# Weights in whole blocks, right halves of the last tiles normalised during P4, rotary loads split from their arithmetic

## The chip, the cores and the metric

The kernel runs on one NeuronCore of a Trainium2 chip. The metric is the device time of one execution in microseconds (us). Three timed executions of the kernel before gave 1953.59, 1955.4 and 1960.35 us; the median is 1955.4 us. The engines are named as in the profile: PE (TensorE matmul), PEld (its weight load), DVE (VectorE), ACT (ScalarE), POOL (GpSimd), SP (SyncE, which here issues most DMAs).

## What is computed

One encoder layer on 1024 tokens of width 1024, in float32, with two half-step feed-forward blocks around a mixer that holds two attentions:

```python
h = h + 0.5 * swiglu(rms_norm(h, ffn1_norm), ffn1_w_gate, ffn1_w_up, ffn1_w_down)
u = rms_norm(h, mix_norm)
z = u @ w_in                      # qA|kA|vA|qB|kB|vB|gA|gB, 4352 columns
qb = rope(qb, pos);  kb = rope(kb, pos)
merged = sigmoid(ga) * (ya @ w_branch_a) + sigmoid(gb) * (yb @ w_branch_b)
h = h + merged @ w_out
h = h + 0.5 * swiglu(rms_norm(h, ffn2_norm), ffn2_w_gate, ffn2_w_up, ffn2_w_down)
y = rms_norm(h, final_norm)
```

`ya` is a neighbourhood attention over a 16 x 64 grid and `yb` a windowed attention with a sink; `rope` turns the first five 128-row chunks of the qB and kB columns by tables of cosine and sine. The feed-forward width is 2816.

## The kernel before

**Arithmetic.** Every large product is made in three matmuls of 128x128 by 128x512 (`mm3`, L137): the operands are split into a high and a low part (`split`, L87: an ACT cast makes the high part, a DVE subtraction the low one), and high-high, high-low and low-high are summed in PSUM. The large matrix products are cut by Strassen's scheme into seven products P1 to P7, each of 12 matmuls per 128 rows of output (4 blocks of the contraction times 3).

**Stages.** `hidden` makes gate, up and their product for the first feed-forward block, `Down` its down projection; the same classes serve `w_out` and the second block. Between them a `transition` normalises the eight token tiles and transposes them. The input projection `w_in` runs as `pg`, with five groups of chunks (`groups`, L850); then the two attentions, with gates, branch products and their loads as filler between the units.

**`products` (L253)** walks through a list `seq` of (group, product, m). For product q it first prepares the weights of some products ahead (`prep_until`, L370: three ahead, up to eight later), then issues the 12 matmuls (`multiply`), then takes the result out of PSUM (`leave`, L382, which calls `store_z` for the input projection) and then calls `at_end(len(seq) - 1 - q)`. For `pg` there are 70 products: P1 and P2 of the first three groups (q = 0 to 11), then P5, P6, P3, P7, P4 of group 0 (q = 12 to 21), of group 1 (22 to 31) and of group 2 (32 to 41), then all seven of groups 3 and 4. Each product name stands twice in a row, for m = 0 and 1. Functions hung on by `hook(n, f)` run after product q = 69 - n.

**Weights.** `w_cols` (L99) reads 128 columns of a weight matrix as it lies in DRAM, so a block of 1024 x 128 comes as 8 pieces of 512 bytes for each of the 128 partitions: 512 KB in 1024 pieces. It serves `load_w` (L102: gates), `hidden` and `pg` (through `fetch` and `fetch_part`, L304 to L308) and `fetch_branch` (L1114: the branch matrices, 512 rows). The matrices `wd1`, `wd2` and `wo` are read in another way (L540), in rows of 512 columns.

**Rotary (`rope`, L910).** One call loads 128 rows of `z_d` into an `xs` tile x, and the same rows with halves of each head exchanged into another one, y, by four DMAs (L918, L921); multiplies x by cosine (L922), y by sine (L923), adds (L924), and stores to `zr_d` from POOL (L925). `xs` has two buffers. The five calls hang at q = 19, 22, 25, 28 and 33. The rows of call 0 are complete in `z_d` after product q = 16, those of calls 1, 2, 3 and 4 after q = 20, 17, 21 and 26. `v_b_load` (L927) hangs at q = 35 and takes an `xs` buffer too, `v_b` at q = 49.

**The end.** `Down.run` (L607) of the last projection takes the products P2, P1, P5, P6, P3, P7, P4 with 11 steps each and yields after each step of P7 and P4. The right halves (columns 512 to 1023) of token tiles 4 to 7 are final after P7, the left halves only after P4. The last five steps of P4 are made tile by tile: `tail(j)` (L626) issues 15 matmuls for one tile and adds the result to its left half (`evict`, L604). After each, `finish` (L1411) normalises the tile: `normed` (L111) with two parts squares each half on ACT with a running sum (L118), adds the two sums (L120), scales and adds epsilon (L121) on DVE, takes the power -1/2 on POOL (L122), multiplies each half by that and the gain on DVE (L124), and SP stores each half (L1415).

**Order of the instructions.** When the program is built, a planner lines the instructions of each engine up, by their place in the program, by their dependences and by its own costs for each instruction and DMA; on the chip each engine then keeps to that line. `pin` (`tc.keep_in_program_order`) forces one instruction behind the one that was issued before it on its engine.

Of the kernel before, what the change touches and what calls it, by code (L numbers as in the profile page):

```python
# [10 lines left out]
F32 = mybir.dt.float32  # L11
F32R = mybir.dt.float32r
AF = mybir.ActivationFunctionType
ALU = mybir.AluOpType

P = 128
T = 1024
D = 1024
# [9 lines left out]
EPS = 1e-6  # L28
# [8 lines left out]
def trunk_kernel(ctx, tc, x, xt, n1c, wg1, wu1, wd1, nm, win, rpb, sink, wa, wb, wo,  # L37
                 n2, wg2, wu2, wd2, nf, c_rope, c_mask_a, c_mask_b, out):
    nc = tc.nc
    x2 = x.rearrange("b t d -> (b t) d")  # L40
    out2 = out.rearrange("b t d -> (b t) d")

    const = ctx.enter_context(tc.tile_pool(name="const", bufs=1))
    main = ctx.enter_context(tc.tile_pool(name="main", bufs=1))
# [5 lines left out]
    def nm_(s):  # L50
        uid[0] += 1
        return f"{s}_{uid[0]}"
# [3 lines left out]
    nhalf = const.tile([P, 1], F32, name="nhalf")  # L56
# [7 lines left out]
    def new_fx(k, dt=F32):  # L64
        fx[k] = main.tile([P, 1024], dt, tag=f"fx{k}", bufs=1, name=nm_("fx"))
        return fx[k]

    def new_ar(g, dt=F32R):
        ar[g] = main.tile([P, 4, 1024], dt, tag=f"ar{g}", bufs=1, name=nm_("ar"))
        return ar[g]  # L70
# [7 lines left out]
    def raw4():  # L78
        return main.tile([P, 1024], F32, tag="raw", bufs=4, name=nm_("raw"))

    def xs4():
        return main.tile([P, 1024], F32, tag="xs", bufs=2, name=nm_("xs"))

    def ws4():
        return main.tile([P, 1024], F32R, tag="ws", bufs=8, name=nm_("ws"))

    def split(dst_hi, dst_lo, src, eng=None):  # L87
        nc.scalar.copy(dst_hi, src)  # L88
        (eng or nc.vector).tensor_tensor(dst_lo, src, f32v(dst_hi), op=ALU.subtract)  # L89

    def load_split(h, l, src_ap, a, b, r=None, eng=None):

        n = a * b
        r = raw4() if r is None else r
        nc.sync.dma_start(r[:, :n].rearrange("p (a b) -> p a b", a=a), src_ap)
        split(h[:, :n], l[:, :n], r[:, :n], eng)
        return (h[:, :n].rearrange("p (a b) -> p a b", a=a), l[:, :n].rearrange("p (a b) -> p a b", a=a))

    def w_cols(w, c0, n=P):  # L99
        return w[:, c0:c0 + n].rearrange("(c p) f -> p c f", p=P)  # L100

    def load_w(w, c0, r=None, eng=None):  # L102

        return load_split(ws4(), ws4(), w_cols(w, c0), w.shape[0] // P, P, r, eng)

    def load_gain(g):
        gb = const.tile([P, 1152], F32, tag="gain", bufs=1, name=nm_("gain"))
        nc.sync.dma_start(gb[:, :D], g.partition_broadcast(P))
        return gb[:, :D]

    def normed(h, gb, xs=None, parts=1):  # L111

        xs = xs4() if xs is None else xs
        w = D // parts
        cols = [slice(i * w, (i + 1) * w) for i in range(parts)]
        st = const.tile([P, 4], F32, tag="st", bufs=4, name=nm_("st"))
        for i, c in enumerate(cols):
            nc.scalar.activation(xs[:, c], h[:, c], AF.Square, accum_out=st[:, i:i + 1])  # L118
        if parts == 2:
            nc.vector.tensor_tensor(st[:, 0:1], st[:, 0:1], st[:, 1:2], op=ALU.add)  # L120
        nc.vector.tensor_scalar(st[:, 0:1], st[:, 0:1], 1.0 / D, EPS, op0=ALU.mult, op1=ALU.add)  # L121
        nc.gpsimd.tensor_tensor(st[:, 2:3], st[:, 0:1], nhalf, op=ALU.pow)  # L122
        for c in cols:
            nc.vector.scalar_tensor_tensor(out=xs[:, c], in0=h[:, c], scalar=st[:, 2:3], in1=gb[:, c],  # L124
                                           op0=ALU.mult, op1=ALU.mult)
        return xs
# [25 lines left out]
    def res(t):  # L152

        return fx[t] if t < 4 else fa[:, (t - 4) * 1024:(t - 3) * 1024]
# [252 lines left out]
    def hidden(wg, wu, at_end, merged=(2,), home=None, unit=None, spill=None, ring=(8, 9, 10, 11, 0, 1, 2, 3, 4, 5, 6, 7)):  # L407
# [12 lines left out]
        def after(i, p, m, bks, snap, sn):  # L420
# [47 lines left out]
            else:  # L468
# [14 lines left out]
                else:  # L483
# [5 lines left out]
                    put(i, "P6", s2)  # L489

        return products(lambda i, m, half: w_cols((wg, wu)[m], (i + half * NP) * P), NP, after, at_end, (6, 7),
                        ring, merged=merged, home=home, spill=spill)

# [198 lines left out]
    pin = tc.keep_in_program_order  # L692
# [43 lines left out]
    def roots(k, total):  # L736

        b = bank("d")
        for j in range(4):
            pin(nc.tensor.matmul(b[:, j * P:(j + 1) * P], total[:, j * P:(j + 1) * P], mean, start=True, stop=True))  # L740
        ms, r = rr[:, 4 * k:4 * k + 4], rr[:, 8 + 4 * k:12 + 4 * k]
        pin(nc.vector.tensor_scalar_add(ms, b.rearrange("p (j t) -> p j t", j=4)[:, :, 0], EPS))
        nc.gpsimd.tensor_tensor(r, ms, nhalf4, op=ALU.pow)
        if k == 0:
            pin(nc.vector.tensor_tensor(rr[:, 16:20], ms, r, op=ALU.mult))
            nc.vector.tensor_scalar_mul(half_r, r, 0.5)
            return r
        pin(nc.vector.tensor_tensor(rr[:, 20:24], r, rr[:, 16:20], op=ALU.mult))
        return rr[:, 20:24]
# [26 lines left out]
    r = roots(0, total)  # L776
# [10 lines left out]
    r = roots(1, total)  # L787
# [58 lines left out]
    gain = load_gain(nm[0])  # L846
    mix = {}
# [3 lines left out]
    NG = len(groups)  # L851
# [55 lines left out]
        nc.sync.dma_start(h_d[t * P:(t + 1) * P, :], res(t))  # L907
        return res(t)

    def rope(k):  # L910

        r0 = (12 + k) * P
        if "rope" not in mix:
            mix["rope"] = [new_fx(i) for i in range(2)]
            for i in range(2):
                nc.sync.dma_start(mix["rope"][i], c_rope[i])
        x, y = xs4(), xs4()
        nc.sync.dma_start(x, z_d[r0:r0 + P, :])  # L918
        for q in range(4):
            o = r0 + 32 * (q ^ 1)  # L920
            nc.sync.dma_start(y[32 * q:32 * q + 32, :], z_d[o:o + 32, :])  # L921
        nc.vector.tensor_tensor(x, x, mix["rope"][0], op=ALU.mult)  # L922
        nc.vector.tensor_tensor(y, y, mix["rope"][1], op=ALU.mult)  # L923
        nc.vector.tensor_tensor(x, x, y, op=ALU.add)  # L924
        nc.gpsimd.dma_start(zr_d[k], x)  # L925
# [71 lines left out]
    def gate_first():  # L997
        mix["gate"] = load_w(win[0], GA + gates[0] * P, xs4())
# [7 lines left out]
    def hook(n, *f):  # L1006
        hooks.setdefault(n, []).append(f)

    for c in range(4):
        hook(14 * (NG - 1) - 6 - 3 * c, rope, c)  # L1010
    hook(14 * (NG - 2) - 6, rope, 4)
    hook(14 * (NG - 2) - 8, v_b_load)
    hook(14 * (NG - 2) - 22, v_b)
    hook(7, q_b, 0)
    hook(6, k_b)
# [1 line left out]
    hook(2, gate_first)  # L1017
    hook(0, keep_u)
    pg = products(lambda i, m, half: w_cols(win[0], groups[i][m][half] * P), NG, store_z, at_end, (2, 3), range(8, 16),
                  ("P1", "P2", "P5", "P6", "P7", "P3", "P4"))  # L1020
    down.into(transition(down1, gain, to_strassen, behind(pg), 2), pg)
# [144 lines left out]
    def filler():  # L1166
        for dc, nxt in zip(gates, gates[1:] + [None]):
            if nxt is not None:
                yield from gate(dc, lambda: mix.update(gate=load_w(win[0], GA + nxt * P)))
            else:  # L1170
                yield from gate(dc, lambda: [load_y(Y_B[c], c * P, nc.gpsimd) for c in range(2)])
        yield from branch_b()
        for i in range(2):
            branch_a(i)
            for _ in range(3):
                drain(a_mm[i][1], 1)
                yield
# [126 lines left out]
    for n in range(1 << 30):  # L1304
# [14 lines left out]
        if n in (59, 60, 61):  # L1319
            c = (59, 60, 61).index(n)  # L1320
# [10 lines left out]
    t = new_ar(2, F32)  # L1331
# [42 lines left out]
    for i, dc in enumerate(a_order):  # L1374
        r = nxt.pop(0)
# [19 lines left out]
    gain = load_gain(n2[0])  # L1395
# [13 lines left out]
    gain = load_gain(nf)  # L1409

    def finish(t):  # L1411
        y = normed(res(t), gain, raw4() if t in (5, 7) else None, 2)
        for n in range(2):
            sl = slice(n * 512, (n + 1) * 512)
            nc.sync.dma_start(out2[t * P:(t + 1) * P, sl], y[:, sl])  # L1415

    for n, _ in enumerate(down.run()):
        if n in (2, 5, 8, 11):
            finish(n // 3)
    for t in range(4, NTT):  # L1420
        down.tail(t - 4)
        finish(t)


def _consts():
# [14 lines left out]
    for cols in ((left, full, right), (full, full, full)):  # L1440
# [7 lines left out]
    return {"c_rope": rope, "c_mask_a": mask_a, "c_mask_b": mask_b}  # L1448


_INS = ['x', 'xt', 'n1c', 'ffn1_w_gate', 'ffn1_w_up', 'ffn1_w_down', 'mix_norm', 'w_in', 'na_rpb', 'sink_logit',
        'w_branch_a', 'w_branch_b', 'w_out', 'ffn2_norm', 'ffn2_w_gate', 'ffn2_w_up', 'ffn2_w_down', 'final_norm']
_OUTS = [((1, 1024, 1024), 'float32')]
# [22 lines left out]
```

## Time and profile before

| | |
|---|---|
| median of 3 executions | 1955.4 us (1953.59 to 1960.35) |
| the profiled execution | 1954.71 us, of which the span of the trace is 1952.9 us |
| PE busy in the span | 1921.4 us (98%) |
| DVE, ACT, POOL busy | 1473.0, 944.5, 337.4 us |
| granted TensorE clock | 0.999 over the span |
| DMA | 297.38 MB, mean 152 GB/s |
| DMA of SP (queue q1) | 214848 packets, 210.17 MB |

The difference of 1.8 us between the profiled execution and its span lies around the trace and is taken as constant. A row of the view of stretches gives the bounds in us, the length, the busy time of the engine with its number of instructions, the granted clock, the mean busy share of the DMA engines (it can exceed 1 where packets overlap) and the rate in GB/s. A row of the view of waits gives who waited for whom, the total in us, how many times, and the longest. A row of the timeline gives start, duration, engine, line, operation, and in brackets the idle time before it and what ended it. A PE row's duration of some 0.39 us is a modelled end; the next matmul starts some 0.23 us after the one before.

### The profile page before, as it was taken

What the parts mean: (1) busy time and instruction counts of PE and PEld (TensorE: products, weight loads), DVE (VectorE), ACT (ScalarE), POOL (GpSimd) and SP (SyncE); (2) the same over time, 40 slices, a digit from 0 to 9 for tenths busy, and PEclk for the clock granted to TensorE, in tenths of its full rate; (3) what the DMA queues carried; (4) which work ended last, traced back from release to release, by engine and by line L of the source; (5) the groups of instructions that cost most, each with busy time, mean ns of one, the idle gap of its engine ahead of it and who ended that gap; (6) DMA issues with size and microseconds to landing.
All of it is one profiled execution on the core that took longest, in us unless ns stands there. A gap on an engine that the chain in (4) does not pass through costs nothing.

```text
span 1952.9 us, 25648 instructions
## 1 busy us (share of the span) xinstructions
PE 1921.4 (98%) x8928; PEld 1597.8 (82%) x8928; DVE 1473.0 (75%) x2606; ACT 944.5 (48%) x1831; POOL 337.4 (17%) x426
## 2 busy tenths in 40 slices
PE   8999999999999999999999999999999999999998
PEld 6778888888888878888888888887888888878886
DVE  6998776668957778678888857999676566559864
ACT  6432333344446543477778863365333333344452
POOL 1011010013400113311122135400111001005200
PEclk9999999999999999999999999999999999999999
DMA  7455333377234489953359566543433323493341
GB/s 228 133 158 173 97 113 107 99 264 254 91 108 135 129 215 245 220 164 95 109 129 203 181 215 217 172 149 92 151 112 118 107 91 108 148 339 106 116 138 59
DMA packets 271521, 297.38 MB, mean 152 GB/s; under 512 B 47360, under 2 KB 200320, under 8 KB 271392
## 3 DMA queue, kind: packets, MB, share of 16 engines
q1 hardware_dynamic: 214848, 210.17, 35.2%
q0 software_dynamic: 56544, 85.58, 15.7%
q8 instruction: 70, 1.15, 0.3%
q14 instruction: 59, 0.48, 0.1%
HBM read 209.09 MB, written 86.70 MB: 151 GB/s over the span
## 4 chain that ended last, share of the span: by engine, by line
PE 78%; issue 9%; DVE 6%; POOL 3%; DMA 2%; ACT 2%; SPq 0%; POOLq 0%; DVEq 0%; ACTq 0%
PE g L140 15%; PE g L142 15%; PE g L144 15%; PE d L140 9%; PE d L142 9%; PE d L144 9%; PE d L1265 2%; POOL zs_d L876 1%; PE g L1279 1%; DVE ws L89 1%; PE g L1284 1%; PE d L1244 1%; PE d L1245 1%; DVE ar L1390 1%; DVE ar L726 1%
## 5 line engine op out<-in xcount | busy, mean ns | idle before, releaser
L140 PE MATMUL g<-ar,ws 128*128 128x512 f32 x1160 | 435.5, 397 | 17.5 <-ACT ar L725 5.9
L142 PE MATMUL g<-ar,ws 128*128 128x512 f32 x1160 | 428.8, 392 | 0.8 <-DVE ar L89 0.4
L144 PE MATMUL g<-ar,ws 128*128 128x512 f32 x1160 | 427.5, 391 | 0.3 <-DVE ws L89 0.3
L89 DVE TENSOR_TENSOR ws<-raw,ws 128x512 fp32r<-128x512 f32 (+1 forms) x339 | 245.5, 729 | 173.6 <-ACT ws L88 171.8
L88 ACT CAST ws<-raw 128x512 fp32r<-128x512 f32 (+1 forms) x341 | 215.1, 637 | 279.3 <-PE d L144 120.0
L140 PE MATMUL d<-ar,ws 128*128 128x512 f32 x704 | 272.2, 390 | 1.2 <-ACT ws L88 1.0
L144 PE MATMUL d<-ar,ws 128*128 128x512 f32 x704 | 271.4, 389 | 0.0
L142 PE MATMUL d<-ar,ws 128*128 128x512 f32 x704 | 271.3, 389 | 0.0
L140 PEld LDWEIGHTS g<-ar,ws 128*128 128x128 f32 x1160 | 213.3, 189 | 59.5 <-DVE fa L900 6.0
L144 PEld LDWEIGHTS g<-ar,ws 128*128 128x128 f32 x1160 | 218.4, 188 | 47.5 <-DVE ws L89 1.1
L142 PEld LDWEIGHTS g<-ar,ws 128*128 128x128 f32 x1160 | 218.4, 188 | 47.5 <-DVE ar L89 0.9
L140 PEld LDWEIGHTS d<-ar,ws 128*128 128x128 f32 x704 | 132.2, 188 | 29.6 <-ACT ws L88 1.8
L144 PEld LDWEIGHTS d<-ar,ws 128*128 128x128 f32 x704 | 132.1, 188 | 27.9 <-DVE ws L89 0.4
L142 PEld LDWEIGHTS d<-ar,ws 128*128 128x128 f32 x704 | 132.2, 188 | 27.1
L418 POOL DMA_DIRECT2D hid<-fx x96 | 52.0, 542 | 420.0 <-DVE fx L481 218.9
L89 DVE TENSOR_TENSOR ws<-ar,ws 128x512 fp32r<-128x512 f32 x114 | 104.9, 927 | 8.8 <-ACT ws L88 8.8
L88 ACT CAST ar<-raw 128x512 fp32r<-128x512 f32 (+1 forms) x83 | 56.0, 678 | 88.8 <-PE g L142 46.4
L140 PE MATMUL g<-ws,ws 128*128 128x512 f32 x232 | 91.0, 392 | 0.1
L142 PE MATMUL g<-ws,ws 128*128 128x512 f32 x232 | 90.4, 390 | 0.0
L144 PE MATMUL g<-ws,ws 128*128 128x512 f32 x232 | 90.3, 389 | 0.0
L1252 ACT ACTIVATE fa<-fa,nmx 128x385 f32<-128x385 f32 (+3 forms) x128 | 75.5, 591 | 26.2 <-DVE nmx L1249 25.5
L89 DVE TENSOR_TENSOR ws<-fa,ws 128x512 fp32r<-128x512 f32 x74 | 51.1, 690 | 47.3 <-ACT ws L88 46.8
(310 smaller groups left out, 3523.5 us busy)
## 6 DMA issues: line engine op xcount, KB each, us to landing
raw<-hid SPq DMA_DIRECT2D x70, 512.0 KB
hid<-fx POOLq DMA_DIRECT2D x96, 256.0 KB, 2.3
raw<-in_ffn_w_up_dram SPq DMA_DIRECT2D x35, 512.0 KB
ar<-in_ffn_w_down_dram SPq DMA_DIRECT2D x32, 512.0 KB
raw<-in_ffn_w_gate_dram SPq DMA_DIRECT2D x31, 512.0 KB
raw<-in_w_in_dram SPq DMA_DIRECT2D x27, 512.0 KB
hid<-fa POOLq DMA_DIRECT2D x51, 256.0 KB, 2.3
ar<-zs_d POOLq DMA_DIRECT2D x48, 256.0 KB, 5.2
```

The lines of the kernel that those rows point to most:

```text
L88: nc.scalar.copy(dst_hi, src)
L89: (eng or nc.vector).tensor_tensor(dst_lo, src, f32v(dst_hi), op=ALU.subtract)
L140: nc.tensor.matmul(b, lhs[0], r[0], start=first, stop=False, **kw)
L142: nc.tensor.matmul(b, lhs[0], r[1], start=False, stop=False, **kw)
L144: nc.tensor.matmul(b, lhs[1], r[0], start=False, stop=last, **kw)
L418: nc.gpsimd.dma_start(hid[PRODUCTS.index(p), i], src)
L726: pin(nc.vector.scalar_tensor_tensor(out=l, in0=src, scalar=scale, in1=f32v(h), op0=ALU.mult, op1=ALU.subtract))
L876: nc.gpsimd.dma_start(dst.rearrange("p b r w -> p b (r w)"), t.rearrange("p (b k) -> p b k", b=NTT))
L1244: nc.tensor.matmul(b[:, :nw], un["q"][s], un["kd"][s][:, k0 * P:k1 * P], start=True, stop=False)
L1245: nc.tensor.matmul(b[:, :nw], un["q"][s], un["kl"][s][:, k0 * P:k1 * P], start=False, stop=True)
L1252: nc.scalar.activation(pr, pr, AF.Exp, scale=-1.0, bias=nmx[:, s:s + 1], accum_out=ssum[:, s:s + 1])
L1265: nc.tensor.transpose(pt[:, i * P:(i + 1) * P], un["pr"][s][:, i * P:(i + 1) * P], ident)
```

## The change

Three edits are made together. The host lays seven weight matrices out so that each block of 128 columns is one stretch of memory in which a partition's row (all its blocks of the contraction) is contiguous; `w_cols` takes such a block. The rotary call is cut into `rope_load` (the DMAs) and `rope` (the arithmetic and the store), hung at q = 19 + 4c and q = 22 + 4c for c = 0 to 4; the first multiplication is pinned; `v_b_load` moves from q = 35 to q = 40. At the end, `begin` for tiles 4 to 7 is called during P4: it squares the right half, scales its sum and adds epsilon, and multiplies the right half by the gain in place. `end` does the rest after the tile's tail: the left half's square, one DVE instruction that scales its sum and adds the other, the power, the left half on DVE and the right half on ACT, and one store from SP and one from ACT's queue, which issued no DMA before.

```diff
-    def w_cols(w, c0, n=P):
-        return w[:, c0:c0 + n].rearrange("(c p) f -> p c f", p=P)
+    def w_cols(w, c0):
+        return w[c0 // P].rearrange("p (c f) -> p c f", f=P)
...
-        return load_split(ws4(), ws4(), w_cols(w, c0), w.shape[0] // P, P, r, eng)
+        return load_split(ws4(), ws4(), w_cols(w, c0), w.shape[-1] // P, P, r, eng)
...
-    def rope(k):
+    def rope_load(k):
 
         r0 = (12 + k) * P
...
-        x, y = xs4(), xs4()
+        x, y = mix["rows"] = xs4(), xs4()
         nc.sync.dma_start(x, z_d[r0:r0 + P, :])
         for q in range(4):
             o = r0 + 32 * (q ^ 1)
             nc.sync.dma_start(y[32 * q:32 * q + 32, :], z_d[o:o + 32, :])
-        nc.vector.tensor_tensor(x, x, mix["rope"][0], op=ALU.mult)
+
+    def rope(k):
+
+        x, y = mix.pop("rows")
+        pin(nc.vector.tensor_tensor(x, x, mix["rope"][0], op=ALU.mult))
         nc.vector.tensor_tensor(y, y, mix["rope"][1], op=ALU.mult)
         nc.vector.tensor_tensor(x, x, y, op=ALU.add)
         nc.gpsimd.dma_start(zr_d[k], x)
...
-    for c in range(4):
-        hook(14 * (NG - 1) - 6 - 3 * c, rope, c)
-    hook(14 * (NG - 2) - 6, rope, 4)
-    hook(14 * (NG - 2) - 8, v_b_load)
+    for c in range(5):
+        hook(14 * (NG - 1) - 6 - 4 * c, rope_load, c)
+        hook(14 * (NG - 1) - 9 - 4 * c, rope, c)
+    hook(14 * (NG - 2) - 13, v_b_load)
...
+    late = {}
+
+    def begin(t):
+
+        y = main.tile([P, 1024], F32, tag="raw" if t % 2 else "xs", bufs=4 if t % 2 else 2, name=nm_("y"))
+        st = const.tile([P, 4], F32, tag="st", bufs=4, name=nm_("st"))
+        h = res(t)[:, 512:]
+        nc.scalar.activation(y[:, 512:], h, AF.Square, accum_out=st[:, 1:2])
+        nc.vector.tensor_scalar(st[:, 1:2], st[:, 1:2], 1.0 / D, EPS, op0=ALU.mult, op1=ALU.add)
+        nc.vector.tensor_tensor(h, h, gain[:, 512:], op=ALU.mult)
+        late[t] = y, st
+
+    def end(t):
+        y, st = late.pop(t)
+        h = res(t)
+        nc.scalar.activation(y[:, :512], h[:, :512], AF.Square, accum_out=st[:, 0:1])
+        nc.vector.scalar_tensor_tensor(out=st[:, 0:1], in0=st[:, 0:1], scalar=1.0 / D, in1=st[:, 1:2],
+                                       op0=ALU.mult, op1=ALU.add)
+        nc.gpsimd.tensor_tensor(st[:, 2:3], st[:, 0:1], nhalf, op=ALU.pow)
+        nc.vector.scalar_tensor_tensor(out=y[:, :512], in0=h[:, :512], scalar=st[:, 2:3], in1=gain[:, :512],
+                                       op0=ALU.mult, op1=ALU.mult)
+        nc.scalar.activation(y[:, 512:], h[:, 512:], AF.Copy, scale=st[:, 2:3])
+        nc.sync.dma_start(out2[t * P:(t + 1) * P, :512], y[:, :512])
+        nc.scalar.dma_start(out2[t * P:(t + 1) * P, 512:], y[:, 512:])
+
     for n, _ in enumerate(down.run()):
         if n in (2, 5, 8, 11):
             finish(n // 3)
+        if 11 < n < 16:
+            begin(n - 8)
     for t in range(4, NTT):
         down.tail(t - 4)
-        finish(t)
+        end(t)
...
+def _blocks(w):
+
+    k, n = w.shape[1:]
+    return w.reshape(k // P, P, n // P, P).transpose(2, 1, 0, 3).reshape(1, n // P, P, k)
+
+
+_BLOCKED = ['ffn1_w_gate', 'ffn1_w_up', 'w_in', 'w_branch_a', 'w_branch_b', 'ffn2_w_gate', 'ffn2_w_up']
...
+    laid.update({name: _blocks(inputs[name]) for name in _BLOCKED})
```

## The prediction

> **What bounds the kernel now.** I read the page first, then PE by stretches of 50 us, then the waits of PE, and only then the timeline of each place where PE loses time.
>
> ```profile
> span 1952.9 us, 25648 instructions
> PE 1921.4 (98%) x8928; PEld 1597.8 (82%) x8928; DVE 1473.0 (75%) x2606; ACT 944.5 (48%) x1831; POOL 337.4 (17%) x426
> ```
> ```profile
> 50.00:100.00 50.00, 48.04 (x206) 1.00 0.45 132
> ...
> 200.00:250.00 50.00, 50.00 (x222) 1.00 0.35 111
> ...
> 700.00:750.00 50.00, 46.35 (x203) 1.00 0.86 217
> 1900.00:1950.00 50.00, 44.16 (x194) 1.00 0.20 65
> ```
> ```profile
> PE g L140 <- ACT ar L725: 5.9, 1, 5.9
> PE g L140 <- DVE fa L900: 4.9, 3, 3.0
> PE g L140 <- DVE fx L471: 2.6, 2, 1.3
> PE g L140 <- DVE fa L455: 2.1, 1, 2.1
> PE d L140 <- ACT ws L88: 1.0, 1, 1.0
> PE g L140 <- ACT ws L88: 1.0, 1, 1.0
> ```
>
> PE is busy for 1921.4 of 1952.9 us, so no edit that leaves its matmuls alone can win more than 31.5 us. Most stretches look like 200:250, full, with 222 matmuls in 50 us: there, nothing in this change is worth anything, since a weight that comes sooner only waits longer. The 31.5 us lie in a few places: 5.9 before the first matmul, about 8.8 at the end (PE stops 5.84 before 1950, and the span ends 2.9 after that), 3.65 in 700:750, 1.96 in 50:100, and single waits of 1.3 for L471 (behind the loads at 116, below) and of 2.1 for L455 (behind those at 1314). So the sum is made place by place. A wait removed from PE moves everything behind it forward, since PE is full after each.
>
> **The end (`begin`, `end`).** The rows are from the timelines of PE, DVE and SP in the last 20 us.
>
> ```profile
> 1933.59 0.39 PE L144 MATMUL g<-ar 128*128 128x512 f32 x1
> ...
> 1943.79 0.39 PE L144 MATMUL g<-ar 128*128 128x512 f32 x1
> ```
> ```profile
> 1934.01 0.69 DVE L604 SCALAR_TENSOR_TENSOR fa<-g,fa 128x512 f32<-128x512 f32 x1 [7.07 <-PE g L144]
> 1935.49 0.16 DVE L120 TENSOR_TENSOR st<-st 128x1 f32<-128x1 f32 x1 [0.79 <-ACT xs L118]
> 1935.69 0.15 DVE L121 TENSOR_SCALAR st<-st 128x1 f32<-128x1 f32 x1
> 1936.60 1.42 DVE L124 SCALAR_TENSOR_TENSOR xs<-fa,st,gain 128x512 f32<-128x512 f32 x2 [0.76 <-POOL st L122]
> ...
> 1945.75 0.69 DVE L604 SCALAR_TENSOR_TENSOR fa<-g,fa 128x512 f32<-128x512 f32 x1
> ```
> ```profile
> 1949.10 0.99 SPq L1415 DMA_DIRECT2D out_dram<-raw  x2
> ```
>
> The first tile's last matmul starts at 1933.59 and the last tile's at 1943.79, so PE needs (1943.79 - 1933.59) / 3 = 3.40 us a tile. DVE needs (1945.75 - 1934.01) / 3 = 3.91, because each tile's eviction stands in its queue behind both L124 of the tile before. So the last eviction starts at 1945.75, although PE allows it at 1934.01 + 3 x 3.40 = 1944.21: 1.54 us are lost. In the new order a tile's DVE chain loses one small instruction (from 1935.49 to 1935.69, 0.20) and the second half of L124 (1.42 for two, so 0.71), which ACT makes at the same time. The chain is then 3.91 - 0.20 - 0.71 = 3.00 us, shorter than PE's 3.40: PE sets the pace, and the 1.54 come back. Behind the last eviction 0.20 goes too, and the second store no longer waits for 0.71 of DVE. Sum 1.54 + 0.20 + 0.71 = 2.45; I take **2.4**.
>
> Unknown is the issue of a DMA from ACT, which this trace doesn't show. SP's two stores of the last tile take 0.99 to issue, so 0.5 each. An issue can't be had for less than nothing, and the half that ACT sends no longer queues for SP, so the term could reach 2.9; an issue twice as dear as SP's at the last tile makes it 1.9. Behind ACT's issue stands the next tile's square, which has 3.40 - 3.00 = 0.4 us to spare and is not late unless the issue takes over 0.9. I take SP's price, as it is the same kind of DMA.
>
> `begin` adds 4 x 0.7 of DVE and 4 short ones, and four squares on ACT, during P4.
>
> ```profile
> 1914.00:1930.00 16.00, 16.00 (x71) 13.25 (x72) 8.02 (x13) 6.25 (x12) 0.00 (x0) 1.00 0.00 1
> ```
>
> In 1914:1930 DVE is busy for 8.02 and ACT for 6.25 of 16 us, so it costs nothing; its inputs come from P7, the product before. Without this cover it would put 4 x 0.7 = 2.8 us back into the end.
>
> **Rotary loads.** Timelines of SP, DVE and PE around the longest of the waits for L900.
>
> ```profile
> 710.77 0.34 SPq L918 DMA_DIRECT2D xs<-z_d  x1
> 716.54 1.23 DVE L922 TENSOR_TENSOR xs<-xs,fx 128x1024 f32<-128x1024 f32 x1 [2.95 <-DMA xs<-z_d]
> 718.43 0.50 PE L140 MATMUL g<-ar,ws 128*128 128x512 f32 x1 [2.96 <-DVE fa L900]
> 723.27 1.22 DVE L924 TENSOR_TENSOR xs<-xs,xs 128x1024 f32<-128x1024 f32 x1
> 728.71 1.23 DVE L922 TENSOR_TENSOR xs<-xs,fx 128x1024 f32<-128x1024 f32 x1 [2.64 <-DMA xs<-z_d]
> 729.94 1.73 SPq L921 DMA_DIRECT2D xs<-z_d  x4
> ...
> 786.44 1.22 DVE L924 TENSOR_TENSOR xs<-xs,xs 128x1024 f32<-128x1024 f32 x1
> ```
>
> This is a wait inside a queue: DVE stands at L922 for 2.95 us for a load issued at 710.77, and behind it stands L900, the eviction of P7, for which PE waits 2.96. Three products are 36 matmuls, at 222 in 50 us 8.1 us; the load took 5.8 (710.77 to 716.54). So at its new place the first multiplication finds its data, and **3.0** us come back. The second wait, 2.64 at 728.71, cost PE nothing: no eviction due at once stood behind it.
>
> What is late next: the calls now come every four products, 10.8 us, through two `xs` buffers, while the five additions L924 were (786.44 - 723.27) / 4 = 15.8 us apart. The exchanged rows of call 1 could only be fetched at 729.94, once the store of call 0 was out. If such a lag reaches the pinned L922 of the fourth or fifth call, DVE waits again, and the fifth stands at q = 38, a P7 once more. But L922 needs only x, whose buffer is free as soon as L924 has read y: it ran at 728.71, 4.2 us after the addition that began at 723.27 had ended. I take no new wait of PE; the bound on the other side is one more stall of the first one's size, so this term is 0 to 3.0, or 3.65 with all that PE loses in 700:750. On SP the five loads of a call stand ahead of the weight loads as before, at later places.
>
> **Weights in blocks.** Rates where the DMA engines are full, and the places where an engine in front of PE waits for such a load.
>
> ```profile
> 108.00:116.00 8.00, 8.00 (x37) 6.64 (x36) 5.75 (x10) 2.52 (x5) 0.29 (x1) 1.00 1.04 285
> 410.00:430.00 20.00, 20.00 (x90) 16.57 (x89) 8.13 (x13) 7.46 (x13) 0.54 (x1) 1.00 1.02 374
> ```
> ```profile
> 95.11 0.69 DVE L327 TENSOR_TENSOR s<-fa 128x512 f32<-128x512 f32 x1 [0.96 <-DMA fa<-in_ffn_w_gate_dram]
> 109.89 0.37 SPq L308 DMA_DIRECT2D fa<-in_ffn_w_up_dram  x1
> 116.44 0.69 DVE L327 TENSOR_TENSOR s<-fa 128x512 f32<-128x512 f32 x1 [2.56 <-DMA fa<-in_ffn_w_up_dram]
> 701.05 0.69 DVE L327 TENSOR_TENSOR s<-fx 128x512 f32<-128x512 f32 x1 [3.40 <-DMA fx<-in_w_in_dram]
> 1314.12 0.62 ACT L88 CAST ws<-ahead 128x512 fp32r<-128x512 f32 x1 [2.21 <-DMA ahead<-in_ffn_w_gate_dram]
> ```
>
> In 108:116 nearly all the traffic is gate and up weights, in pieces of 512 bytes, and full engines move 285 GB/s. In 410:430, where most of it is rows of 2 KB and longer, they move 374. At that rate a load in a full queue needs 285 / 374 = 0.76 of its time; rows of 4 KB may do better. The load of 109.89 landed at 116.44, after 6.55 us, so it comes about 1.6 us sooner. A load that is alone in the queue gains only its own 524 KB at 285 against 374 GB/s, 1.84 - 1.40 = 0.44 us.
>
> Place by place: the wait at 116.44 shrinks from 2.56 to 1.0, and PE's wait of 1.3 for L471 behind it goes (**1.3**). The 0.96 at 95.11 goes, and with it PE's 1.0 for the cast (**1.0**). At 701.05 DVE gets some 1.6 of its 3.40 us earlier, which takes away most of the 0.7 that PE loses in 700:750 besides the 2.96 (3.65 in all; **0.5**). Around 1314 the two loads are nearly alone, so 0.7 of the 2.21 go, and of PE's 2.1 behind them **0.7**. At the start the 1.0 for the cast behind the first loads may halve, and the 5.9 may shrink (**0.4**; bounds 0 and 1.5). Sum **3.9**. The lower bound is 0, if PE waits for DVE's backlog at all these places and not for the load; the upper, all the waits named taken away whole, 1.0 + 2.6 + 0.7 + 2.1 + 1.5 = 7.9.
>
> [...]
>
> **Sum.** 2.4 + 3.0 + 3.9 = 9.3 us. Against the profiled execution (span 1952.9 and 1.8 around it, 1954.7) that is 1945.4; that execution lies 0.7 below the median of 1955.4, so as a median I forecast **1946.1**.
>
> **Rivals.**
> - *The blocks move no wait of PE.* Either pieces of 512 bytes cost no more than rows here, or the host's layout still arrives in pieces because the pattern of eight blocks isn't joined, or DVE's own work is what PE waits for in 50:150. For: DVE is short of time there, with a wait of 0.96 at 95.11 among work without gaps. Against: 285 against 374 GB/s, and waits that end with the load. Time 1955.4 - 2.4 - 3.0 = 1950.0.
> - *The rotary calls give back what they win.* One new stall at a P7, of the size of the old: 1955.4 - 2.4 - 3.9 = 1949.1. For: 15.8 us between additions against 10.8 between calls. Against: x is there 4.2 us after the addition.
> - *Slower: the two `xs` buffers set the pace.* If a call can't be done in less than the 15.8 us seen, DVE, which now keeps L922 in its place among the evictions, falls behind by 5.0 a call, 20 by the fifth; 2.6 of that is free once (the wait at 728.71). PE loses 17.4: 1955.4 - 9.3 + 17.4 = 1963.5. It decides where a call needs over 13 us, since 4 x (13.1 - 10.8) = 9.3 eats the gain. Against: the 15.8 was no need; calls hung 3 and 5 products apart and lay among other work, L922 to L924 alone taking 8 us of the first.
>
> **How the numbers follow.** A measurement of this kernel can tell about 0.3%, 5.9 us, from no change. The forecast has 0.57; the blocks without effect 0.22; the rotary giving back 0.12; the slower rival 0.06; 0.03 is left for an order by the planner that costs time elsewhere. Faster by more than 5.9 us (below 1949.5) are nearly all of the first and about half of the third: 0.64. Within: the second, most of the rest of the third and the edge of the first, 0.28. Slower: 0.08. The range reaches down to 1942, the ends of the terms that can go up together (0.5 from the end, 0.6 from the rotary, 3.0 of the 4.0 that lie between 3.9 and 7.9 of the weights, 1955.4 - 13.4), and up to 1951.5, which holds both milder rivals and the end at 1.9.
>
> **What would show it.** In the page: packets under 2 KB fall to a third or less, and PE's busy time stays near 1921. At the end: evictions L604 3.4 us apart, and the span ending some 6.4 us after the last of them. Around 715: no wait of DVE at the first rotary multiplication; look then at the fourth and fifth and at the evictions behind them. In 50:150: no PE wait for L471; if full engines there still move 285 GB/s, the blocks failed; if they move 374 or more and PE waits as before, DVE was the cause. The prediction is wrong if a rotary multiplication ahead of a P7 eviction waits for over 3 us, or if the planner's new order makes PE wait where it was full.

## The result and the profile after

| | before | after |
|---|---|---|
| median of 5 executions each, one chip | 1953.59 us (1951.76 to 1960.35) | 1943.55 us (1941.87 to 1944.78) |
| ratio, 95% interval | | 0.9942 [0.9923, 0.9960] |
| profiled execution, its span | 1954.71, 1952.9 us | 1941.87, 1940.1 us |

The change takes 10.0 us off the medians; 9.3 was forecast, and 1943.55 lies in the range. The agreement hides two terms that came out wrong and make up for each other, as the experiments show: that the total agrees is luck. First the page of after, in the order in which before was read: PE's busy time is nearly what it was, and packets under 2 KB went from 200320 to a quarter of that.

```profile
span 1940.1 us, 25638 instructions
...
PE 1918.4 (99%) x8928; PEld 1597.1 (82%) x8928; DVE 1472.6 (76%) x2606; ACT 948.6 (49%) x1835; POOL 336.5 (17%) x426
...
DMA packets 140961, 297.38 MB, mean 153 GB/s; under 512 B 47360, under 2 KB 48768, under 8 KB 140832
```

PE by stretches of after (bounds, length, PE busy, clock, DMA share, GB/s), then its longest waits:

```profile
8.00:14.00 6.00, 6.00 (x24) 1.00 1.04 389
50.00:100.00 50.00, 49.24 (x214) 1.00 0.43 142
100.00:150.00 50.00, 50.00 (x222) 1.00 0.47 170
106.00:110.00 4.00, 4.00 (x19) 1.00 0.99 391
700.00:750.00 50.00, 49.48 (x218) 1.00 0.90 247
```
```profile
PE g L140 <- ACT ar L725: 6.1, 1, 6.1
PE g L140 <- DVE fa L455: 1.4, 1, 1.4
...
PE g L140 <- DVE fa L900: 0.8, 1, 0.8
...
PE g L140 <- DVE fa L898: 0.5, 1, 0.5
PE g L140 <- DVE fa L471: 0.4, 1, 0.4
```

Full DMA engines now move 389 GB/s in 8:14, where nearly all packets are of 2 KB (weights and token columns), and 391 in 106:110, where they are of 4 KB, weights alone. PE loses 0.52 us in 700:750 instead of 3.65 and nothing in 100:150. The two waits for `fx` at L471, 2.6 together, are gone (the 0.4 for `fa` is not among them), and that for L455 is 1.4 instead of 2.1.

PE issues the same 8928 matmuls in both kernels, so the n-th starts can be subtracted. The table gives, by place, how much of the lead over before's profiled execution each execution gains there; the last three kernels are experiments below.

| matmuls, place | forecast | after | blocks alone | without the rotary edit | rotary loads swapped |
|---|---|---|---|---|---|
| to the 73rd, start | 0.4 | 2.16 | 1.00 | 1.61 | 1.25 |
| to the 481st, 50 to 125 us | 2.3 | 3.15 | 3.34 | 3.22 | 3.04 |
| to the 2929th, 665 us | 0 | 0.67 | 0.47 | 1.02 | 1.13 |
| to the 3501st, 700 to 800 us | 3.5 | 3.33 | 2.80 | 0.28 | 4.00 |
| to the 5785th | 0 | -0.12 | -0.04 | -0.14 | -0.58 |
| to the 6217th, 1314 us | 0.7 | 0.67 | 0.74 | 0.59 | 0.69 |
| to the 7993rd, 1725 us | 0 | 1.39 | 1.60 | 1.62 | 1.51 |
| from there to the end of the span | 2.4 | 1.59 | 0.02 | 1.58 | 1.57 |
| sum | 9.3 | 12.84 | 9.93 | 9.78 | 12.61 |

The 1.4 to 1.6 at 1725 us belong to the execution of before: two experiments that leave that place untouched, the end alone and the rotary edit alone, gain 1.62 and 1.61 there too. So about 1.5 of the 12.84 is no gain. The same holds for a part of two other rows: three executions with nearly all weights as before (the end alone, the rotary edit alone, the first eight loads alone) stand 0.5 to 1.3 ahead of before's at 50 to 125 us and 0.2 to 0.4 at 1314 us.

**The end.** Timelines of DVE, SP and ACT's queue in after:

```profile
1922.76 0.69 DVE L604 SCALAR_TENSOR_TENSOR fa<-g,fa 128x512 f32<-128x512 f32 x1 [7.11 <-PE g L144]
...
1932.96 0.69 DVE L604 SCALAR_TENSOR_TENSOR fa<-g,fa 128x512 f32<-128x512 f32 x1 [0.28 <-PE g L144]
1934.44 0.16 DVE L1437 SCALAR_TENSOR_TENSOR st<-st 128x1 f32<-128x1 f32 x1 [0.79 <-ACT y L1436]
1935.33 0.75 DVE L1440 SCALAR_TENSOR_TENSOR y<-fa,st,gain 128x512 f32<-128x512 f32 x1 [0.73 <-POOL st L1439]
```
```profile
1936.08 0.37 ACTq L1444 DMA_DIRECT2D out_dram<-y  x1
```

The evictions stand (1932.96 - 1922.76) / 3 = 3.40 us apart, PE's pace, and each waits for PE. But the span ends 1940.1 - 1932.96 = 7.1 us after the last one, as before (1952.9 - 1945.75 = 7.1).

**The rotary part.** Timelines of DVE and SP in after:

```profile
711.21 1.23 DVE L927 TENSOR_TENSOR xs<-xs,fx 128x1024 f32<-128x1024 f32 x1 [0.80 <-DMA xs<-z_d]
...
714.30 1.23 DVE L928 TENSOR_TENSOR xs<-xs,xs 128x1024 f32<-128x1024 f32 x1
...
779.48 1.22 DVE L928 TENSOR_TENSOR xs<-xs,xs 128x1024 f32<-128x1024 f32 x1
```
```profile
715.55 0.33 SPq L918 DMA_DIRECT2D xs<-z_d  x1
...
721.78 1.72 SPq L921 DMA_DIRECT2D xs<-z_d  x4
```

The planner put the sine product (L927) of the first call ahead of the pinned cosine product, and the wait there is 0.80 instead of 2.95. The five additions L928 are still (779.48 - 714.30) / 4 = 16.3 us apart, no closer than the 15.8 of before.

### The profile page after: what moved, and what is told of

It is laid out like the page before. It is cut to its first block, busy times and chain, and to the rows that moved or that the text cites. A ratio compares the mean times of both kernels' runs of the same rounds, so it can differ in the third digit from the quotient of the medians.

```text
span 1940.1 us, 25638 instructions
## 1 busy us (share of the span) xinstructions
PE 1918.4 (99%) x8928; PEld 1597.1 (82%) x8928; DVE 1472.6 (76%) x2606; ACT 948.6 (49%) x1835; POOL 336.5 (17%) x426
## 4 chain that ended last, share of the span: by engine, by line
PE 82%; DVE 6%; issue 5%; DMA 3%; ACT 2%; POOL 1%; SPq 0%; POOLq 0%; DVEq 0%; ACTq 0%
PE g L140 16%; PE g L142 16%; PE g L144 16%; PE d L144 10%; PE d L140 10%; PE d L142 10%; PE d L1269 2%; PE d L1248 1%; PE g L1288 1%; PE d L1249 1%; PE g L1283 1%; DVE ws L89 1%; DVE ar L1394 1%; DMA z_d<-fa 1%; DVE ar L726 1%
```

## The experiments

All ratios are to before, measured on the same chip. My theory after the result was that each edit does what the forecast said, with the start undervalued; the rivals were that the blocks alone had done the rotary edit's work, and that the start is more than the arrival of weights.

**One edit at a time.** Three kernels are before with one hunk of the diff each. A fourth is before with only the first eight weight loads taken from an extra input laid out in blocks:

```diff
-            fetch_part(r, i, m, k)
+            nc.sync.dma_start(r, w_first[i, m][:, k * 512:k * 512 + 512])
```

> The kernel before with the block layout alone. Theory A (the edits are independent, each pays at its own places): PE's instruction of the same number comes about 2.2 us sooner from the first 30 us on, 5.3 after 120 us, 6.0 after 670 us; the wait of DVE at the first rotary multiplication and PE's wait of about 3 for L900 behind it stay; in all 7 to 9 us, about 1945. Theory B (the rotary wait is only a late effect of slow w_in loads): that wait goes with the blocks alone, and the gain is 10 to 12 us.

Measured: 1946.94 us against 1954.47, ratio 0.9963 [0.9951, 0.9975], 7.5 us less. PE's long wait in the rotary part is down to 1.1 with the rotary code as it was (SP, DVE, PE):

```profile
704.45 0.33 SPq L918 DMA_DIRECT2D xs<-z_d  x1
```
```profile
708.93 1.22 DVE L922 TENSOR_TENSOR xs<-xs,fx 128x1024 f32<-128x1024 f32 x1 [1.36 <-DMA xs<-z_d]
```
```profile
710.81 0.50 PE L140 MATMUL g<-ar,ws 128*128 128x512 f32 x1 [1.10 <-DVE fa L900]
```

The load takes 708.93 - 704.45 = 4.5 us from its issue instead of 5.8, and DVE reached the place with 1.3 us less delay, since its wait for a `w_in` load there is 2.15 at 695.02 instead of 3.40 at 701.05. The time is that of theory A, the shorter wait is nearer to B. Over all traces with the rotary code as it was, the load takes 5.4 to 6.2 us in four executions with the weights as before and PE waits 2.5 to 3.5; with the blocks it takes 4.5 and 4.8 and PE waits 1.1 and 1.8. So the blocks pay in the rotary part too. That they do so by shortening what the rotary loads queue with fits these times; no run isolates it.

> The kernel before with begin and end alone. Theory A: everything up to the tail as before; evictions L604 of the last four tiles 3.40 us apart in place of 3.91; the span 1.5 to 1.7 us shorter, not the 2.4 of the prediction, because the two stores of the last tile need the same time for their bytes, however they are issued. Rival (the tail's shortfall in the changed kernel came from the blocks or the rotary edit): 2.4 us shorter.

Measured: 1953.53 us against 1954.47, 0.9998 [0.9989, 1.0008]. The time can't tell 1.6 us from nothing here, the trace can: from the start of the last matmul to the end of the span it is 7.55 us, against 9.16 in before, in the blocks alone and in the rotary edit alone, and 7.57 in after. So the end is worth 1.6.

> The kernel before with the rotary split alone. Theory A: DVE's 2.95 at the first rotary multiplication goes and with it PE's 2.96 for L900; 2.5 to 3.5 us shorter, less up to 0.8 for new short waits at later calls. Theory B (slow w_in loads are the root): the wait moves and less than 1 us is won.

Measured: 1955.56 us against 1954.47, 1.0010 [1.0000, 1.0021]: the rotary edit by itself wins nothing. Its trace shows what became of the 3 us. PE by stretches, then DVE and PE around the second call, then DVE, SP and PE around the fourth:

```profile
700.00:720.00 20.00, 19.57 (x87) 1.00 0.81 222
720.00:740.00 20.00, 18.62 (x83) 1.00 0.71 176
740.00:760.00 20.00, 19.69 (x87) 1.00 1.42 301
760.00:780.00 20.00, 18.46 (x81) 1.00 1.08 212
```
```profile
728.69 0.69 DVE L327 TENSOR_TENSOR s<-fx 128x512 f32<-128x512 f32 x1 [2.02 <-DMA fx<-in_w_in_dram]
```
```profile
740.31 0.50 PE L140 MATMUL g<-ar,ws 128*128 128x512 f32 x1 [1.68 <-DVE fa L898]
```
```profile
755.52 1.23 DVE L928 TENSOR_TENSOR xs<-xs,xs 128x1024 f32<-128x1024 f32 x1
...
762.13 1.23 DVE L926 TENSOR_TENSOR xs<-xs,fx 128x1024 f32<-128x1024 f32 x1 [2.27 <-DMA xs<-z_d]
```
```profile
756.77 0.34 SPq L918 DMA_DIRECT2D xs<-z_d  x1
```
```profile
772.54 0.50 PE L140 MATMUL g<-ar,ws 128*128 128x512 f32 x1 [1.28 <-DVE fa L898]
```

PE loses 0.43 in 700:720, where before lost 3.65, and then 1.38, 0.31 and 1.54: 3.66 in all.

The first new wait, at 740.31, is not for rotary rows. DVE waits 2.02 us for a `w_in` load at 728.69 and then works without a gap until the eviction that PE awaits, with the second call's three instructions (1.2 us each) among the evictions. In all six executions with the edited rotary code and its loads in this order PE's wait here is DVE's wait for that `w_in` load less 0.34 us: 0.52 after 0.86 in after, 0.58 after 0.92, 0.62 after 0.96, 0.74 after 1.08, 1.68 after 2.02 here, 2.54 after 2.88.

The second is the one that the prediction named. The load three products ahead is issued at 756.77, the moment at which the third call's addition ends (755.52 + 1.23) and its buffer comes free, not when its hook stands in the program. It lands 5.4 us later, the pinned L926 waits 2.27, DVE then has no gap for 13 us, and PE waits 1.28 for an eviction at 772.54. The time is theory B's (less than 1 us won), but not by its cause: the wait at the first call did go.

> The kernel before, with only the first eight weight loads (gate and up of the first two column blocks, 256 KB each) taken from an extra copy in block layout; the other weights as before. Theory A (the first matmuls run at half pace until PE has been busy without a gap for some 3.7 us, and the 1.0 gap at 7.9 made that phase start again): the gap goes, matmuls reach 0.23 us apart at about 10 in place of 14.2, and PE is 2.0 to 2.6 us ahead after 30 us, from the same 1.0 us of waiting removed. Rival (the gap alone counts): 0.4 to 1.0 us ahead.

Measured: 1955.50 us against 1954.47, 1.0006 [0.9996, 1.0015]. In its profile the first matmul came 1.9 us later than in before, held by another load (the column of `n1c`), so it says nothing on the arrival of weights. The 73rd was 0.31 earlier nonetheless, with no gap among the first matmuls and the half pace lasting from 7.8 to 12.8; that pointed at PE itself.

**The start.** In both kernels the first matmuls stand 0.43 us apart and later ones 0.23. Two kernels put 17 matmuls on a tile of ones ahead of the first real one, in after and in before:

```diff
+    warm = main.tile([P, 512], F32, tag="hs", bufs=4, name="warm")[:, :P]
+    nc.vector.memset(warm, 1.0)
+    wb_ = ps.tile([P, 512], F32, tag="d", name="wps")
+    for k in range(17):
+        nc.tensor.matmul(wb_[:, k % 4 * P:(k % 4 + 1) * P], warm, warm, start=True, stop=True)
     hg[4](0, 0, 0)
```

> The changed kernel with 17 matmuls of 128x128 on a tile set to ones, queued ahead of the first real matmul. Clock theory (the half pace of the first matmuls, 0.427 us against 0.23, is TensorE's own and ends once it has been busy for some 3.7 us): the first real matmuls run 0.23 apart, and the 73rd stands 0.8 to 1.8 us earlier than the 26.59 - 2.16 = 24.42 us of the changed kernel, less what the 17 matmuls (3.9 us at full pace, 7.3 at half) delay the first; the time falls by 0.5 to 1.8 us. Rival (the first matmuls go at the pace at which the weights arrive): the spacing stays, the 73rd is within 0.3 us of 24.42, and the time is the same.

> The kernel before with the same 17 matmuls ahead of its first one. Clock theory: of the 8.3 us that the kernel before runs at half pace (5.88 to 14.19), what its loads allow comes back: the 73rd matmul at 24 to 25.5 us instead of 26.59, and 1 to 2.5 us less in all. Were all of the 2.16 us that the blocks gain at the start their earlier landing, it would stay at 26.3 to 26.9, and the time within 0.3 us.

Measured: before with them 1951.77 us against 1954.39, 0.9987 [0.9975, 0.9998]; after with them 1943.79 (four executions), 0.9945 [0.9926, 0.9964]. PE's first rows, of before with the 17 (the trace has 34 records for them), of after with the 17, and of after:

```profile
1.05 6.70 PE L706 MATMUL wps<-warm 128*128 128x128 f32 x34 [1.05 <-DVE warm L703]
7.50 0.47 PE L140 MATMUL g<-ar,ws 128*128 128x512 f32 x1
7.82 0.39 PE L142 MATMUL g<-ar,ws 128*128 128x512 f32 x1
8.04 0.40 PE L144 MATMUL g<-ar,ws 128*128 128x512 f32 x1
```
```profile
1.05 5.44 PE L706 MATMUL wps<-warm 128*128 128x128 f32 x34 [1.05 <-DVE warm L703]
```
```profile
7.89 0.74 PE L140 MATMUL g<-ar,ws 128*128 128x512 f32 x1
8.43 0.63 PE L142 MATMUL g<-ar,ws 128*128 128x512 f32 x1
8.86 0.65 PE L144 MATMUL g<-ar,ws 128*128 128x512 f32 x1
9.31 0.63 PE L140 MATMUL g<-ar,ws 128*128 128x512 f32 x1
9.74 0.45 PE L142 MATMUL g<-ar,ws 128*128 128x512 f32 x1
10.03 0.39 PE L144 MATMUL g<-ar,ws 128*128 128x512 f32 x1
10.25 0.39 PE L140 MATMUL g<-ar,ws 128*128 128x512 f32 x1
```

In before with the 17, real matmuls go 0.23 to 0.34 apart from the first on, but for one step of 0.49; from 8.87 on all go at 0.23, where before without them goes at 0.43 until 14.2, with the same loads. The 73rd stands at 24.39 us in before with them (26.59 without) and at 23.47 in after with them (24.42 without). So the half pace is PE's own, not the weights', though the profile's clock column shows 1.00 for 8:14 in both kernels. How long it lasts is another matter. In after it ends 3.7 us after the first matmul (from 6.08 to 9.74), which is the 3.7 of the expectations, but over the six executions without the 17 that have no wait above 0.1 us among the first matmuls it lasts 3.6 to 6.5 us (5.0 with the first eight loads, 6.5 with the blocks alone); in before, with a wait of 0.99 that ends at 8.88, and in two others with waits of 0.93 and 1.58 it lasts 8.2 to 8.8. So no fixed time is shown. That such a gap prolongs it fits this; that the gap starts the same 3.7 us again does not, since in before the half pace goes on for 5.3 us behind it. What sets its length within the 3.6 to 6.5 is not shown.

How much of the blocks' gain at the start is earlier data isn't settled either. With the 17 in both, the blocks put the 73rd 24.39 - 23.47 = 0.9 us earlier, but in before the 17 themselves took 6.70 us and in after 5.44, so some of the 0.9 can be theirs. The gain without them, 1.0 to 2.2 in the four executions of the table, goes with the end of the half pace: 9.7 us where it is 2.16, 12.7 where it is 1.00.

In the profiled execution of after with the 17, the lead was lost at the rotary part: 11.16 us at the 3121st matmul, 4.94 at the 3501st. PE waited 2.54 us at the second call, behind DVE's 2.88 for the `w_in` load, went at half pace for another 1.0 (granted clock 0.83 in 730:740), and waited 1.3 us after DVE's 3.82 for the rows of the fourth. So 1 us won at the start didn't show in the time, which the expectation had missed.

**The end's missing 0.8 us.** One kernel stores both halves from SP. Another leaves out the store of the last tile's right half.

```diff
-        nc.scalar.dma_start(out2[t * P:(t + 1) * P, 512:], y[:, 512:])
+        nc.sync.dma_start(out2[t * P:(t + 1) * P, 512:], y[:, 512:])
```
```diff
+        if t < 7:
             nc.scalar.dma_start(out2[t * P:(t + 1) * P, 512:], y[:, 512:])
```

> The changed kernel with the right half of each of the last four tiles stored from SyncE's queue instead of ScalarE's. Transfer theory (the 512 KB of the last tile's two stores set the end, whichever queue issues them): last eviction to end of span 7.0 to 7.5 us, as the 7.18 of the changed kernel. Rival (the store on ScalarE's queue is late, since it stands behind the last scaling there, and keeps the second half's 0.71 us from coming back): below 6.7.

> The changed kernel without the store of the last tile's right half (columns 512 to 1023 of the last 128 rows are not written). Transfer theory: half of the 1.85 us in which the last 512 KB move goes away, so last eviction to end of span 6.1 to 6.5 us instead of 7.18. Rival (a fixed time from a store's issue to the end, whatever it moves): 7.0 to 7.2.

Measured, in one execution of each, the last eviction (both from SP, then one store left out):

```profile
1934.84 0.69 DVE L604 SCALAR_TENSOR_TENSOR fa<-g,fa 128x512 f32<-128x512 f32 x1 [0.28 <-PE g L144]
...
1937.95 0.33 SPq L1444 DMA_DIRECT2D out_dram<-y  x1
1938.38 0.38 SPq L1443 DMA_DIRECT2D out_dram<-y  x1
```
```profile
1935.48 0.69 DVE L604 SCALAR_TENSOR_TENSOR fa<-g,fa 128x512 f32<-128x512 f32 x1 [0.28 <-PE g L144]
```

The spans are 1941.8 and 1941.9 us, so 7.0 and 6.4 us remain behind the eviction, against 7.1. Which queue issues hardly mattered (0.2 less, a little under the expected range); half the bytes less was worth 0.7 (7.1 - 6.4). So the bytes of the last tile count behind its scaling. In before, the first half was issued at 1949.10 while DVE scaled the second for 0.71; with both halves ready together the same 512 KB still follow, which fits that taking those 0.71 away shortened nothing.

**The rotary edit on top of the blocks.** One kernel is the whole change without the rotary hunk. One swaps the two loads, so that the four small ones go into the buffer that comes free first, and pins the sine product instead:

```diff
-        x, y = mix["rows"] = xs4(), xs4()
-        nc.sync.dma_start(x, z_d[r0:r0 + P, :])
+        y, x = mix["rows"] = xs4(), xs4()
         for q in range(4):
...
             nc.sync.dma_start(y[32 * q:32 * q + 32, :], z_d[o:o + 32, :])
+        nc.sync.dma_start(x, z_d[r0:r0 + P, :])
```

The third is the whole change once more.

> The kernel before with the weights in blocks and with the halves of the last four tiles, and without the edit of the rotary loads. Theory (with the blocks the wait of 2.96 us at the rotary part is down to 1.1 by itself, as the blocks alone showed, so the rotary edit is worth at most 0.6 us on top of them, and what it wins at its first product it can lose at the later ones): the same time as the whole change within 1 us. Rival (the rotary edit brings its 3 us on top of the blocks): 2.5 to 3 us longer than the whole change.

> The whole change with the two rotary loads in the other order: the four loads of 32 rows first, into the buffer that comes free with the sum, and the one load of 128 rows second, into the buffer that comes free only when the rotated rows are stored. Theory (the two buffers set the pace of the rotary tiles: the second load stands behind the store of the tile before, some 6.2 us after its sum, and then takes 1.72 us to issue): the second load takes 0.33 us to issue instead of 1.72, the tiles follow 1 to 1.4 us closer, the waits of DVE for rotary rows between 700 and 790 us fall from the 3.9 us of the whole change to under 2, and PE's waits there stay under 0.6; the time is at most 1 us shorter. Rival (the loads' own way, not their issue, sets the pace): the waits stay at 3 to 5 us.

> The whole change once more, beside the two others on one chip: 1943.5 us, within 1 us, by the five runs that there are. Its profile shows how far two executions of one kernel differ at 700 to 800 us: 0.5 us of waits of PE there if the first was typical, up to 4 if the loss there comes from when the rotary loads land in that execution.

Measured, against 1954.13: without the rotary edit 1944.79 us, 0.9946 [0.9932, 0.9959]; the whole change 1944.79, 0.9953 [0.9940, 0.9966], 1.2 above the 1943.55 of its first measurement; swapped 1942.11, 0.9935 [0.9922, 0.9948]. The rotary edit adds nothing to the medians. PE in the kernel without it, and its stretch with the clock in the column before the last two:

```profile
708.33 0.39 PE L144 MATMUL g<-ar,ws 128*128 128x512 f32 x1
710.49 0.50 PE L140 MATMUL g<-ar,ws 128*128 128x512 f32 x1 [1.77 <-DVE fa L900]
...
711.54 0.63 PE L140 MATMUL g<-ar,ws 128*128 128x512 f32 x1
711.96 0.63 PE L142 MATMUL g<-ar,ws 128*128 128x512 f32 x1
```
```profile
710.00:715.00 5.00, 4.51 (x13) 0.66 0.77 267
```

After a wait of 1.77 us, eight matmuls go at 0.43 again, another 1.6 us, with a granted clock of 0.66 from 710 to 715: that is how this execution kept only 0.28 of the place. So the edit trades a wait of 1 to 2 us at the first call, sometimes with a half pace behind it, for mostly smaller ones later on, and its balance can't be told from the times. The traces of all experiments together give what PE loses between 690 and 800 us, counted by how much further apart than 0.227 us its matmuls start:

| weights | rotary code | loss in each profiled execution, us |
|---|---|---|
| as before | as before | 4.3, 4.8, 5.2, 6.8 |
| as before | edited | 4.8 |
| blocks | as before | 1.5, 3.9 |
| blocks | edited | 0.9, 1.1, 1.2, 1.5, 6.3 |
| blocks | edited, loads swapped | 0.3, 0.3 |

DVE and SP in the swapped kernel, where L920 is the four small loads and L921 the single one:

```profile
715.54 1.23 DVE L928 TENSOR_TENSOR xs<-xs,xs 128x1024 f32<-128x1024 f32 x1
...
770.00 1.22 DVE L928 TENSOR_TENSOR xs<-xs,xs 128x1024 f32<-128x1024 f32 x1
```
```profile
717.79 2.25 SPq L920 DMA_DIRECT2D xs<-z_d  x4
720.37 0.34 SPq L921 DMA_DIRECT2D xs<-z_d  x1
```

The additions are (770.00 - 715.54) / 4 = 13.6 us apart instead of 16.3, closer by 2.7 where 1 to 1.4 was expected, and PE has no wait from 690 to 800. So the order in which the two buffers come free bears on the pace: in after, the second load stands 6.25 us behind the addition (721.78 - 715.53) until the rotated rows are stored, and then needs 1.72 us of issue. My number for DVE failed: it still waits 3.5 us for rotary rows, as the rival had it, not under 2, but with no eviction due behind it. PE's wait at the second call is gone with DVE's wait for the `w_in` load, which this order of the instructions doesn't have. The medians differ by 2.7 us, more than the 1 us that I had allowed, and the five executions (1940.62 to 1943.39) all lie below the six of the whole change (1943.60 to 1949.35); the traces place 0.6 to 1.2 of it here, against four of the five in the table, and the rest is not located.

**Both together**, the 17 matmuls and the swapped loads:

> The whole change with both: the 17 matmuls ahead of the first real one, and the four loads of 32 rows ahead of the load of 128 rows. Theory (the lead of 1.0 us that the 17 matmuls gave at the 73rd matmul was lost at 700 to 800 us, where the rotary loads' landing decides, and with the loads in the other order that place no longer depends on it): no wait of PE over 0.6 us at 700 to 800, the lead over the kernel before at the 73rd matmul 3 to 3.6 us and kept to the end, the time 0.5 to 1.5 us below the 1942.1 of the kernel with the swapped loads alone. Rival (a lead at the start is eaten wherever a later load is awaited): 1942.1 within 0.4 us.

Measured: 1940.24 us (1937.69 to 1941.54) against 1954.28, 0.9928 [0.9915, 0.9942], the shortest of all. The lead is 2.97 at the 73rd matmul, 10.78 at the 3501st and 13.09 at the last; PE has no wait from 690 to 800. It lies 1.9 us below the swapped loads alone, a little more than expected; that was measured on another chip, and the intervals overlap. In the trace the lead of the start is kept this time: 1.7 us over the swapped loads alone at the 73rd matmul, 2.1 at the last.

## Why the prediction was right, and where it was not

**Weights, 3.9 forecast, 7.5 measured.** The mechanism held: 389 to 391 GB/s in full engines, no wait of PE behind the loads at 116 us, a shorter one behind 1314. At 50 to 125 us it was 3.0 to 3.3 instead of 2.3, which agrees once one takes off the 0.5 to 1.3 by which executions without the blocks are ahead of before's there; at 1314 it was 0.6 to 0.7 as forecast, of which by the same reckoning 0.2 to 0.4 are no gain. Two sizes were off. At the start it was 1.0 to 2.2 instead of 0.4: how long the half pace lasts counts there, which the forecast did not see, although the rows of before had 0.43 between matmuls. And the rotary place gained 2.8 from the blocks alone, where the step allowed 0.5 (0.3 in the execution without the rotary edit, whose wait had the half pace behind it): it took the stall at L922 for a load issued too late, though with the blocks, and the code as it was, 1.1 and 1.8 were left of the 2.96.

**Rotary, 3.0 forecast, about nothing measured.** The step that failed is "I take no new wait of PE". It asked only whether x is there at the pinned product, and two waits came in place of the old one. At the second call DVE waits for a `w_in` load and then has the call's three instructions to do among the evictions: PE waits 1.68. At the fourth, x's buffer is indeed free as soon as the addition has read y, but the load is only issued then and lands 5.4 us later, when the call is already due: PE waits 1.28. The rival that the rotary calls give back what they win described the second of these, with the place ("the fourth or fifth call"), and the size of both together (one stall of 3 us). The rival of the two buffers had the pace right, 16 us, and the price wrong: DVE has slack (busy for 13.9 to 17.5 of each 20 us from 700 to 780, in after and in the rotary edit alone), so PE lost 4.8 us in the rotary edit alone and 6.3 in the worst execution of the whole change (the one with the 17 matmuls), not 17.4.

**End, 2.4 forecast, 1.6 measured.** The 1.54 for PE's pace came back whole. The 0.20 + 0.71 behind the last eviction did not: the mis-sized term took DVE for what ends the span, while with half of the last tile's bytes left out the 7.1 us went to 6.4. The unknown issue on ACT's queue took 0.37, within the bounds taken from SP.

**The sum.** 1.6 + 7.5 + 0 = 9.1, against 9.3 forecast and medians of 10.0 and 9.3 (1954.13 - 1944.79) in two comparisons. It was right by luck: the blocks did the work that was put down to the rotary edit. The rival in which the blocks move no wait of PE would have the blocks alone at 1.0; they gave 0.9963 [0.9951, 0.9975], and it falls.

## What to carry to other kernels

A wait behind a load can be shortened from two ends, by an earlier issue and by a less crowded queue; when one change does both, the gains overlap and may not be added. Here the blocks alone brought PE's wait of 2.96 us to 1.1, the rotary edit alone to 0.4, and with the blocks the median was 1944.79 us with the rotary edit and without it. A load moved ahead in the program was issued only when its buffer was free (at 756.77, the end of the addition that had read the buffer): read the buffer's last reader and the store behind it before counting the products in between, and give the buffer that comes free last the load that is quickest to issue (0.34 us against 1.72 here, and the additions came 13.6 us apart instead of 16.3). Arithmetic kept in its place among evictions can add to a wait that comes before it, whatever the load: DVE's wait of 2.02 us for a `w_in` load, with the second call's three instructions behind it, became 1.68 of PE's. Behind the last arithmetic the bytes of the last stores counted (7.1 us with 512 KB, 6.4 with 256), so a scaling of 0.71 that ran beside the first of them was not worth its own duration.

## What the runs showed of the hardware

- A PE wait cost more than itself in some executions. In 4 of 14 profiled executions PE went back to 0.43 us a matmul within some 5 us of a wait in the rotary part (1.77 us in the kernel without the rotary edit), for some 5 to 8 matmuls, 1.0 to 1.6 us (in one of them once more at 1110 us, after a wait of 2.39); in others waits of the same kind, up to 3.5, had no such tail (before's 2.96, for one, with 0.23 to 0.24 between the matmuls after 718.77). Here the clock column shows it (0.66 in 710:715 of the kernel without the rotary edit); at the start of the kernel, where the spacing is the same, it does not (1.00 in 8:14).
- Places that no edit touches differ by 1 to 2 us between the profiled executions (1725 us above, 1100 and 1230 us in the kernel with the first eight loads), and in that kernel they add up to 5.6 us between the 3501st and the 5785th matmul. So a term of this size is read from the length of its own stretch, and from more than one execution, not from the time.
